# Two projections of a sparse-attention layer: from three 256-wide matmuls per weight block to one 512-wide and one 256-wide

## The chip, the cores and the metric

One core of a Trainium2 chip runs the kernel. The metric is the device time of one execution in microseconds; three runs of the kernel before took 584.46, 584.71 and 585.03 us, so the median is 584.71 us. All of a time's digits come from such runs or from one execution that was taken with the hardware profiler.

## The reference

The program is a two-layer decoder trunk on 256 tokens of width 1024, all in float32. Layer 0 is an mLSTM layer. Its output gives one set of keys and values, and layer 1 is a sparse-attention layer that reads them. The change touches only layer 1, which computes, for 16 heads of width 128:

```python
h = rmsnorm(x, norm_pre[1])                       # 256 x 1024
proj = h @ w_in                                   # w_in: 1024 x (2048 + 48 + 6144)
q = proj[..., :nqk] * DK ** -0.5                  # 16 heads x 128
gates = sigmoid(proj[..., nqk:nqk + ngl])         # 3 branches x 16 heads
zg = silu(proj[..., nqk + ngl:])                  # 3 branches x 16 heads x 128
# for each branch b (compressed, selected, window) and head:
s = q @ k_b.T - slope[head] * dist                # dist = query position - key position
p = softmax(where(mask, s, -inf))
o = sum over b of gates[b] * zg[b] * (p @ v_b)
x = x + rmsnorm(o @ w_out, norm_post[1])
```

Every matrix product has to keep float32 accuracy. The kernel gets it by splitting both operands into a high part `hi` (rounded to the matmul's own format, F32R) and a low part `lo` (the rest), and adding three products: hi x hi, hi x lo, lo x hi.

## The kernel before

**Tiles.** Activations are kept transposed. `hB` holds rmsnorm(x) for layer 1 as two tiles of 128 x 8 x 256, `hB_hi` and `hB_lo`: 8 blocks of 128 input features, 256 tokens. A projection (`proj_t`, L144) makes 256 output features, that is two halves m of 128, one for each head of a pair, in one PSUM tile `ps` of 128 x 2 x 256. It goes through 2 halves x 8 feature blocks, and for each block `mm3` (L135) issues three matmuls of 256 columns: weights hi with `hB_hi` (L137), weights hi with `hB_lo` (L138), weights lo with `hB_hi` (L139). That makes 48 matmuls a projection.

**Weights.** `w_chunk` (L141) fetches 512 KB by the SP queue into `raw` (4 buffers), ScalarE copies it to `whi` (L132, 5 buffers), VectorE subtracts to `wlo` (L133, 4 buffers). A projection uses two such chunks.

**Layer 1.** There are 8 pairs of heads p, and for each one q projection (`q_proj`, L807, its PSUM tile is `qps`) and three z projections (`z_branch`, L860, `zps`): 32 projections in all. The q and z of pair 0 are made early, among the work on keys and values; those of pair p + 1 are made while pair p goes through its scores, its transposes and its product with the values. On TensorE one pair is the sequence: scores of head 0 (`sps`, 9 matmuls), z projection, scores of head 1, z projection, q projection, 14 transposes of the probabilities (`ptc`, `pt`), z projection, product with the values (`oc`, `ob`, 13 matmuls). After the last pair the output projection (`acc`) follows.

**What follows a projection.** For z, ScalarE reads all 512 columns of `ps` and writes tanh(ps/2) to `zz` (L863); VectorE makes (zz + 1) * ps (L864). For q, ScalarE writes `qhi` (L811) and VectorE `qlo` (L812). A projection holds one of the 3 buffers of the pool `pj` until both are done.

**Softmax of one head** (`softmaxes`, L815). GpSimd makes a table `al` = -slope * dist of 128 x 800 for each head (L823, 2 buffers, 16 in all). VectorE adds it to each of six segments of scores and takes the maximum `mx` at the same time (L836), then `nm` = -mx (L839). ScalarE takes exp(e + nm) with its row sum `sm` (L844). VectorE makes the factors `rsm` (L846 to L849) and scales `e` (L857). The transposes read `e`.

**What sets the order.** The kernel is written with a tile framework: a scheduler puts the instructions of each engine in one list by priority and data dependences, and each engine works through its list in order. A waiting instruction therefore holds up all that stands behind it on its engine.

Of the kernel before, what the change touches and what calls it, by code (L numbers as in the profile page):

```python
# [7 lines left out]
F32 = mybir.dt.float32  # L8
# [7 lines left out]
P = 128  # L16
# [4 lines left out]
def trunk(ctx: ExitStack, tc: tile.TileContext, x, norm_pre, norm_post, a_w_in, a_conv_w, a_conv_b,  # L21
# [155 lines left out]
    def norm_t(t, rstd, gam, hT):  # L177

        n = tp.tile([P, D], F32, tag="tmp", name="nrm")
        for q in range(KT // 4):  # L180
# [63 lines left out]
    with ExitStack() as actx:  # L244
# [349 lines left out]
        for t, n in op.finish():  # L594
# [18 lines left out]
            if t == 0:  # L613
                hB = new_hT("hB")
# [5 lines left out]
    with ExitStack() as bctx:  # L620
# [25 lines left out]
        for c0, base in ((0, 0), (P + NB, 0), (W0, 0), (W0 + P, P), (W0 + 2 * P + NB, P), (W0 + 3 * P + NB, 0)):  # L646
            seg = dist[:, c0:c0 + P]
            nc.gpsimd.iota(seg, pattern=[[-1, P]], base=base, channel_multiplier=1,
                           allow_small_or_imprecise_dtypes=True)
            if base == 0:  # L650
                nc.gpsimd.affine_select(out=seg, in_=seg, pattern=[[-1, P]], compare_op=ALU.is_ge,
                                        fill=MASKED, base=0, channel_multiplier=1)
        for c0, base in ((P, 0), (W0 + 2 * P, P)):
            seg = dist[:, c0:c0 + NB]
            nc.gpsimd.iota(seg, pattern=[[-16, NB]], base=base, channel_multiplier=1,
                           allow_small_or_imprecise_dtypes=True)
            nc.gpsimd.tensor_scalar(seg, seg, -15.5, None, op0=ALU.add)
            nc.gpsimd.affine_select(out=seg, in_=seg, pattern=[[-16, NB]], compare_op=ALU.is_ge,
                                    fill=MASKED, base=base - 31, channel_multiplier=1)
# [116 lines left out]
        def branch_gates():  # L776
# [30 lines left out]
        def q_proj(p):  # L807
            ps = proj_t(bw, p * 256, hB, "qps")
            q = [qz.tile([P, 2, S], F32R, tag=f"q{s}", name=f"q{s}{p}") for s in ("hi", "lo")]
            sc = float(DK) ** -0.5  # L810
            nc.scalar.activation(q[0], ps, AF.Copy, scale=sc)  # L811
            nc.vector.scalar_tensor_tensor(q[1], ps, sc, q[0].bitcast(F32), op0=ALU.mult, op1=ALU.subtract)  # L812
            return q

        def softmaxes(p, q):  # L815
# [3 lines left out]
            for j in range(2):  # L819
                h = 2 * p + j  # L820
                al = b2.tile([P, W0 + KW], F32, tag="al", name=f"al{h}")
                with tc.issue_after(after_norm):
                    nc.gpsimd.tensor_scalar(al, dist, -slopes[h], None, op0=ALU.mult)  # L823
                e = E[:, j, :]
                mx = col(6, "mx")
                for t in range(NT):
# [203 lines left out]
```

## Time and profile before

| | us |
|---|---|
| median of 3 runs (lowest to highest) | 584.71 (584.46 to 585.03) |
| the profiled execution | 583.27 |
| its span, first to last instruction | 581.4 |
| TensorE busy (share of the span) | 568.1 (98%) |
| VectorE busy | 453.1 (78%) |
| ScalarE busy | 311.9 (54%) |
| GpSimd busy | 90.2 (16%) |

The profiled execution is 1.44 us below the median of the runs, and 1.87 us of it lie outside the span. The mean granted clock of TensorE was 0.996 of full speed. Matmuls overlap in the profile: a matmul of 256 columns is listed with about 0.28 us, but the next one starts about 0.12 us later, so what a matmul costs is read from start to start and not from its listed length. VectorE's instructions overlap by some 0.07 us in the same way. Layer 1's projections run from about 264 us on; from 311 us to 515 us seven pairs of heads follow one another, one in 29.1 us.

### The profile page before, as it was taken

How to read it: one execution, taken by the hardware profiler on the slowest of the kernel's cores; microseconds unless marked ns; L12 is line 12 of the kernel's file. 1: busy time of each engine (PE TensorE's matmuls, PEld its weight loads, DVE VectorE, ACT ScalarE, POOL GpSimd, SP SyncE). 2: the span in 40 equal slices, each digit the busy share in tenths (PEclk: the TensorE clock that was granted, in tenths of full speed). 3: DMA queues.
4: the chain of work that ended last, by engine and by line, in shares of the span. 5: the costliest groups of instructions: out<-in, count | busy, mean ns of one | idle time of the engine just before them, and what ended most of it. 6: DMA issues, size and time to landing. Idle time of an engine off the chain costs nothing.

```text
span 581.4 us, 10616 instructions
## 1 busy us (share of the span) xinstructions
PE 568.1 (98%) x4043; PEld 519.1 (89%) x4043; DVE 453.1 (78%) x944; ACT 311.9 (54%) x585; POOL 90.2 (16%) x104
## 2 busy tenths in 40 slices
PE   7998999999999999999999999999999999999995
PEld 3987987989999988879899999999999999998884
DVE  7689887486888876686635789888988998988663
ACT  6475675535544445463334574747474747475521
POOL 7610000201010040130003202021202121210000
PEclk9999999999999999999999999999999999999998
DMA  9984763253422447688995553636374636354501
GB/s 262 227 274 156 241 199 128 74 179 112 145 62 86 144 145 253 203 267 263 289 300 163 149 148 108 182 109 183 108 181 110 183 109 183 109 182 149 202 11 73
DMA packets 82693, 96.69 MB, mean 166 GB/s; under 512 B 4811, under 2 KB 68449, under 8 KB 82642
## 3 DMA queue, kind: packets, MB, share of 16 engines
q1 hardware_dynamic: 81040, 92.48, 52.0%
q0 software_dynamic: 1600, 3.52, 2.8%
q8 instruction: 32, 0.52, 0.4%
q14 instruction: 19, 0.16, 0.1%
q10 hardware_dynamic: 2, 0.00, 0.0%
HBM read 94.94 MB, written 1.05 MB: 165 GB/s over the span
## 4 chain that ended last, share of the span: by engine, by line
PE 90%; DVE 6%; issue 1%; DMA 1%; ACT 1%; POOL 0%; DVEq 0%; POOLq 0%; ACTq 0%
PE zps L137 11%; PE zps L139 11%; PE zps L138 11%; PE acc L137 5%; PE acc L138 5%; PE acc L139 5%; PE qps L138 3%; PE qps L137 3%; PE qps L139 3%; PE o L137 2%; PE o L138 2%; PE o L139 2%; PE pt L869 2%; DVE wlo L133 2%; PE xmps L139 1%; PE xmps L138 1%
## 5 line engine op out<-in xcount | busy, mean ns | idle before, releaser
L133 DVE TENSOR_TENSOR wlo<-raw,whi 128x1024 fp32r<-128x1024 f32 x150 | 181.6, 1222 | 62.5 <-PE zps L139 22.3
L132 ACT ACTIVATE whi<-raw 128x1024 fp32r<-128x1024 f32 x151 | 157.5, 1053 | 122.0 <-issue 27.1
L137 PE MATMUL zps<-hB_hi,whi 128*128 128x256 f32 x384 | 109.5, 285 | 0.0
L138 PE MATMUL zps<-hB_lo,whi 128*128 128x256 f32 x384 | 108.6, 283 | 0.0
L139 PE MATMUL zps<-hB_hi,wlo 128*128 128x256 f32 x384 | 108.6, 283 | 0.0
L823 POOL TENSOR_SCALAR al<-dist 128x800 f32<-128x800 f32 x16 | 42.4, 2647 | 209.8 <-DVE mx L836 159.6
L137 PEld LDWEIGHTS zps<-hB_hi,whi 128*128 128x128 f32 x384 | 73.5, 191 | 0.8 <-issue 0.8
L139 PEld LDWEIGHTS zps<-hB_hi,wlo 128*128 128x128 f32 x384 | 73.6, 192 | 0.0
L138 PEld LDWEIGHTS zps<-hB_lo,whi 128*128 128x128 f32 x384 | 73.6, 192 | 0.0
L844 ACT ACTIVATE e<-e,nm 128x16 f32<-128x16 f32 (+2 forms) x96 | 37.7, 394 | 16.3 <-DVE nm L839 15.9
L139 PE MATMUL xmps<-hA_hi,wlo 128*128 128x256 f32 x128 | 36.7, 287 | 3.5 <-DVE wlo L133 3.3
L137 PE MATMUL xmps<-hA_hi,whi 128*128 128x256 f32 x128 | 36.3, 283 | 0.5 <-ACT whi L132 0.5
L137 PE MATMUL zps<-hA_hi,whi 128*128 128x256 f32 x128 | 36.6, 286 | 0.0
L139 PE MATMUL zps<-hA_hi,wlo 128*128 128x256 f32 x128 | 36.4, 284 | 0.0
L138 PE MATMUL zps<-hA_lo,whi 128*128 128x256 f32 x128 | 36.3, 283 | 0.0
L137 PE MATMUL qps<-hB_hi,whi 128*128 128x256 f32 x128 | 36.2, 283 | 0.0
L138 PE MATMUL qps<-hB_lo,whi 128*128 128x256 f32 x128 | 36.2, 283 | 0.0
L139 PE MATMUL qps<-hB_hi,wlo 128*128 128x256 f32 x128 | 36.2, 283 | 0.0
L138 PE MATMUL xmps<-hA_lo,whi 128*128 128x256 f32 x128 | 36.2, 283 | 0.0
L139 PEld LDWEIGHTS xmps<-hA_hi,wlo 128*128 128x128 f32 x128 | 24.5, 191 | 4.5 <-DVE wlo L133 4.5
L137 PEld LDWEIGHTS xmps<-hA_hi,whi 128*128 128x128 f32 x128 | 24.5, 192 | 1.0 <-ACT whi L132 0.8
L137 PE MATMUL o<-whi,hA_hi 128*128 128x512 f32 x64 | 25.3, 395 | 0.0
(338 smaller groups left out, 1416.7 us busy)
## 6 DMA issues: line engine op xcount, KB each, us to landing
raw<-in_b_w_in_dram SPq DMA_DIRECT2D x64, 512.0 KB, 4.8
raw<-in_a_w_in_dram SPq DMA_DIRECT2D x48, 512.0 KB, 4.6
raw<-in_a_w_out_dram SPq DMA_DIRECT2D x16, 512.0 KB, 3.7
w<-in_cmp_w_dram SPq DMA_DIRECT2D x32, 256.0 KB, 6.6
raw<-in_b_w_out_dram SPq DMA_DIRECT2D x16, 512.0 KB, 3.6
raw<-in_kv_w_dram SPq DMA_DIRECT2D x8, 512.0 KB, 7.5
raw<-in_kv_w_dram SPq DMA_DIRECT2D x8, 256.0 KB, 3.7
x<-in_x_dram SPq DMA_DIRECT2D x4, 256.0 KB, 3.7
```

What stands on the lines that cost most here:

```text
L132: a = nc.scalar.activation(hi, src, AF.Copy)
L133: return a.ins, nc.vector.tensor_sub(lo, src, hi.bitcast(F32)).ins
L137: nc.tensor.matmul(dst, lhsT=l[0], rhs=r[0], start=start, stop=False)
L138: nc.tensor.matmul(dst, lhsT=l[0], rhs=r[1], start=False, stop=False)
L139: last_mm[0] = nc.tensor.matmul(dst, lhsT=l[1], rhs=r[0], start=False, stop=stop).ins
L823: nc.gpsimd.tensor_scalar(al, dist, -slopes[h], None, op0=ALU.mult)
L844: nc.scalar.activation(e[:, c0:c0 + n], e[:, c0:c0 + n], AF.Exp, bias=nm[:, i:i + 1], accum_out=sm[:, i:i + 1])
L869: nc.tensor.transpose(dst, E[:, j, c0:c0 + P], ident)
```

## The change

`hB` becomes two tiles by feature blocks instead of two tiles by part: `hB[q]` is 128 x 4 x 2 x 256, and for each feature block the high and the low part stand side by side as 512 columns. A new generator `proj_pairs` multiplies the high weights with all 512 columns in one matmul and then adds the low weights times the high part to the first 256. The PSUM tile of one half m now has 128 x 2 x 256: the first 256 columns hold hi x hi + lo x hi, the second hi x lo, and someone has to add the two. ScalarE copies the second to SBUF, VectorE adds the first. The generator hands out one half at a time, so each is evacuated by itself. z's last two steps go to GpSimd as a product and a sum. The q of each head is divided by the head's slope; then `dist` (now with its sign turned) can be added to the scores of every head, the multiplication by -slope is part of VectorE's reducing instruction, which takes a minimum, and `al` and the step from `mx` to `nm` are gone.

```diff
+    def proj_pairs(w, c0, hP, name):
+        ch = [w_chunk(w, 0, c0), w_chunk(w, 4, c0)]
+        for m in range(2):
+            ps = pjt([P, 2, S], name)
+            for c in range(2):
+                for k in range(4):
+                    l = [ch[c][i][:, k, m * P:(m + 1) * P] for i in range(2)]
+                    r = hP[c][:, k]
+                    nc.tensor.matmul(ps.rearrange("p i s -> p (i s)"), lhsT=l[0], rhs=r.rearrange("p i s -> p (i s)"),
+                                     start=c + k == 0, stop=False)
+                    last_mm[0] = nc.tensor.matmul(ps[:, 0], lhsT=l[1], rhs=r[:, 0], start=False,
+                                                  stop=c + k == 4).ins
+            yield m, ps
...
         def q_proj(p):
-            ps = proj_t(bw, p * 256, hB, "qps")
             q = [qz.tile([P, 2, S], F32R, tag=f"q{s}", name=f"q{s}{p}") for s in ("hi", "lo")]
-            sc = float(DK) ** -0.5
-            nc.scalar.activation(q[0], ps, AF.Copy, scale=sc)
-            nc.vector.scalar_tensor_tensor(q[1], ps, sc, q[0].bitcast(F32), op0=ALU.mult, op1=ALU.subtract)
+            for j, ps in proj_pairs(bw, p * 256, hB, "qps"):
+                sc = float(DK) ** -0.5 / slopes[2 * p + j]
+                qs = qz.tile([P, S], F32, tag="half", bufs=3, name="qs")
+                nc.scalar.activation(qs, ps[:, 1], AF.Copy)
+                nc.vector.tensor_add(qs, ps[:, 0], qs)
+                nc.scalar.activation(q[0][:, j, :], qs, AF.Copy, scale=sc)
+                nc.vector.scalar_tensor_tensor(q[1][:, j, :], qs, sc, q[0][:, j, :].bitcast(F32),
+                                               op0=ALU.mult, op1=ALU.subtract)
...
-                al = b2.tile([P, W0 + KW], F32, tag="al", name=f"al{h}")
-                with tc.issue_after(after_norm):
-                    nc.gpsimd.tensor_scalar(al, dist, -slopes[h], None, op0=ALU.mult)
...
-                        nc.vector.tensor_tensor_reduce(e[:, c0:c0 + n], src, al[:, c0:c0 + n], 1.0, -1e30,
-                                                       ALU.add, ALU.max, mx[:, 3 * t + b:3 * t + b + 1])
-                nm = col(6, "nm")
-                nc.vector.tensor_scalar(nm, mx, -1.0, None, op0=ALU.mult)
+                        nc.vector.tensor_tensor_reduce(e[:, c0:c0 + n], src, dist[:, c0:c0 + n], -slopes[h], 1e30,
+                                                       ALU.add, ALU.min, nm[:, 3 * t + b:3 * t + b + 1])
...
                         nc.scalar.activation(e[:, c0:c0 + n], e[:, c0:c0 + n], AF.Exp, bias=nm[:, i:i + 1],
-                                             accum_out=sm[:, i:i + 1])
+                                             scale=-1.0, accum_out=sm[:, i:i + 1])
...
         def z_branch(b, p):
-            ps = proj_t(bw, NQK + NGL + b * NQK + p * 256, hB, "zps")
             zz = qz.tile([P, 2, S], F32, tag="zz", bufs=6, name=f"zz{b}_{p}")
-            nc.scalar.activation(zz, ps, AF.Tanh, scale=0.5)
-            nc.vector.scalar_tensor_tensor(zz, zz, 1.0, ps, op0=ALU.add, op1=ALU.mult)
+            for j, ps in proj_pairs(bw, NQK + NGL + b * NQK + p * 256, hB, "zps"):
+                z = zz[:, j, :]
+                nc.scalar.activation(z, ps[:, 1], AF.Copy)
+                nc.vector.tensor_add(z, ps[:, 0], z)
+                th = qz.tile([P, S], F32, tag="half", bufs=3, name="zth")
+                nc.scalar.activation(th, z, AF.Tanh, scale=0.5)
+                nc.gpsimd.tensor_mul(th, th, z)
+                nc.gpsimd.tensor_add(z, z, th)
             return zz
```

The pieces left out make `hB` with the new shape (`new_pairs`, `norm_t`, `branch_gates`) and turn the sign of `dist`.

On TensorE and on the SP queue the order of the work stays the same, apart from the matmuls inside the 32 projections. On VectorE the list of a pair changes. This piece of the list before stands between the score maxima of head 1 and the transposes; `wlo` is a weight chunk's low part, `ec` and `e` are the scaled probabilities that the transposes read.

```order
L133 TENSOR_TENSOR wlo_4152<-raw_4149,whi_4151 128x1024
L839 TENSOR_SCALAR nm<-mx 128x6
L133 TENSOR_TENSOR wlo_4246<-raw_4243,whi_4245 128x1024
L133 TENSOR_TENSOR wlo_4252<-raw_4249,whi_4251 128x1024
L846 TENSOR_SCALAR sm<-sm 128x6
L848 RECIPROCAL rsm<-sm 128x6
L849 TENSOR_TENSOR rsm<-rsm,gs 128x6
L864 SCALAR_TENSOR_TENSOR zz_2_4139<-zz_2_4139,zps 128x512
L857 TENSOR_SCALAR ec_3933<-e_3932,rsm 128x3x16
L857 TENSOR_SCALAR e_3932<-e_3932,rsm 128x128 x2
L857 TENSOR_SCALAR ec_3933<-e_3932,rsm 128x3x16
L857 TENSOR_SCALAR e_3932<-e_3932,rsm 128x256 x2
```

The same place on VectorE now (lines of the changed file; L887 is the sum of a z half):

```order
L133 TENSOR_TENSOR wlo_4083<-raw_4080,whi_4082 128x1024
L868 TENSOR_SCALAR sm<-sm 128x6
L870 RECIPROCAL rsm<-sm 128x6
L887 TENSOR_TENSOR zz_2_4013<-zps,zz_2_4013 128x256
L871 TENSOR_TENSOR rsm<-rsm,gs 128x6
L133 TENSOR_TENSOR wlo_4169<-raw_4166,whi_4168 128x1024
L879 TENSOR_SCALAR ec_3881<-e_3880,rsm 128x3x16
L879 TENSOR_SCALAR e_3880<-e_3880,rsm 128x128 x2
L879 TENSOR_SCALAR ec_3881<-e_3880,rsm 128x3x16
L879 TENSOR_SCALAR e_3880<-e_3880,rsm 128x256 x2
L133 TENSOR_TENSOR wlo_4175<-raw_4172,whi_4174 128x1024
L887 TENSOR_TENSOR zz_2_4013<-zps,zz_2_4013 128x256
```

`nm` has left the list; of the three `wlo` ahead of `sm`, two now stand behind `rsm`, one of them behind the scaled `e`; and the `zz` of a whole projection has become two sums of halves, the second behind the scaled `e`. On ScalarE this is the list before from the exponentials of head 0 on; `whi` is a weight chunk's high part:

```order
L844 ACTIVATE e_4332,sm<-e_4332,nm 128x16
L844 ACTIVATE e_4332,sm<-e_4332,nm 128x128 x2
L844 ACTIVATE e_4332,sm<-e_4332,nm 128x16
L844 ACTIVATE e_4332,sm<-e_4332,nm 128x256 x2
L863 ACTIVATE zz_3_4435<-zps 128x512
L132 ACTIVATE whi_4551<-raw_4549 128x1024
L132 ACTIVATE whi_4645<-raw_4643 128x1024
L132 ACTIVATE whi_4651<-raw_4649 128x1024
```

and this the list now, where `zth` is the tanh of a half and waits for VectorE's sum of it:

```order
L866 ACTIVATE e_4250,sm<-e_4250,nm 128x16
L866 ACTIVATE e_4250,sm<-e_4250,nm 128x256 x2
L886 ACTIVATE zz_3_4288<-zps 128x256
L132 ACTIVATE whi_4452<-raw_4450 128x1024
L132 ACTIVATE whi_4538<-raw_4536 128x1024
L889 ACTIVATE zth<-zz_3_4288 128x256
L886 ACTIVATE zz_3_4288<-zps 128x256
L866 ACTIVATE e_4250,sm<-e_4250,nm 128x16
L889 ACTIVATE zth<-zz_3_4288 128x256
L866 ACTIVATE e_4250,sm<-e_4250,nm 128x128 x2
```

Where ScalarE had one instruction for a z projection it now has four, in two pairs, each with a VectorE instruction between its two. GpSimd's list loses its 16 `al` and gets 96 instructions of 128 x 256, a product and a sum for each of 48 z halves.

## Rows read from the trace of the kernel before

**Rows 1.** The page's busy times of the engines over the span.
```profile
PE 568.1 (98%) x4043; PEld 519.1 (89%) x4043; DVE 453.1 (78%) x944; ACT 311.9 (54%) x585; POOL 90.2 (16%) x104
```

**Rows 2.** The chain of waits, shares of the span by engine.
```profile
PE 90%; DVE 6%; issue 1%; DMA 1%; ACT 1%; POOL 0%; DVEq 0%; POOLq 0%; ACTq 0%
```

**Rows 3.** One pair: stretch, span, busy of PE, PEld, DVE, ACT, POOL, clock, DMA.
```profile
369.60:398.70 29.10, 29.10 (x240) 28.79 (x239) 26.00 (x67) 17.84 (x42) 5.58 (x2) 1.00 0.50 144
```

**Rows 4.** TensorE in order of time: start, listed length, line, output<-inputs, shape.
```profile
376.88 0.39 PE L137 MATMUL ob<-pt00hi,V0hi 128*128 128x512 f32 x1
...
377.58 0.28 PE L137 MATMUL ob<-pt1hi,V1hi 128*128 128x256 f32 x1
...
377.93 0.40 PE L137 MATMUL ob<-pt01hi,V0hi 128*128 128x512 f32 x1
...
378.64 0.28 PE L137 MATMUL ob<-pt1hi,V1hi 128*128 128x256 f32 x1
...
380.11 0.28 PE L137 MATMUL zps<-hB_hi,whi 128*128 128x256 f32 x1
...
385.86 0.29 PE L137 MATMUL sps<-KThi,qhi 128*128 128x272 f32 x1
...
558.05 0.39 PE L137 MATMUL acc<-whi,yThi 128*128 128x512 f32 x1
...
562.95 0.39 PE L137 MATMUL acc<-whi,yThi 128*128 128x512 f32 x1
```

**Rows 5.** Groups by line and shape: count, busy us, mean ns of one, idle before.
```profile
L864 DVE SCALAR_TENSOR_TENSOR zz<-zz,zps 128x512 f32<-128x512 f32 x24 | 16.3, 680 | 0.1
L839 DVE TENSOR_SCALAR nm<-mx 128x6 f32<-128x6 f32 x16 | 10.5, 657 | 0.1
L463 DVE SCALAR_TENSOR_TENSOR xc<-xc,vec,zth 128x256 f32<-128x256 f32 x16 | 7.7, 480 | 0.0
L812 DVE SCALAR_TENSOR_TENSOR qlo<-qps,qhi 128x512 fp32r<-128x512 f32 x8 | 5.5, 690 | 3.2 <-ACT qhi L811 3.2
L491 DVE TENSOR_TENSOR dd<-dps,cmask 128x256 f32<-128x256 f32 x4 | 1.7, 415 | 0.0
...
L863 ACT ACTIVATE zz<-zps 128x512 f32<-128x512 f32 x24 | 13.9, 578 | 0.0
L728 ACT ACTIVATE rs<-R 128x256 f32<-128x256 f32 x2 | 0.8, 378 | 1.0 <-PE R L721 1.0
```

**Rows 6.** VectorE in order of time, around work of GpSimd and away from it.
```profile
158.32 0.48 DVE L463 SCALAR_TENSOR_TENSOR xc<-xc,vec,zth 128x256 f32<-128x256 f32 x1
...
159.44 0.29 DVE L524 TENSOR_SCALAR rd<-rd 128x2 f32<-128x2 f32 x1
...
181.57 0.16 DVE L524 TENSOR_SCALAR rd<-rd 128x2 f32<-128x2 f32 x1
...
324.25 0.17 DVE L839 TENSOR_SCALAR nm<-mx 128x6 f32<-128x6 f32 x1
...
382.97 0.69 DVE L133 TENSOR_TENSOR ylowlo<-yacc,ylowhi 128x512 fp32r<-128x512 f32 x1
383.58 0.82 DVE L839 TENSOR_SCALAR nm<-mx 128x6 f32<-128x6 f32 x1
```

**Rows 7.** GpSimd in order of time at the same places.
```profile
158.47 1.23 POOL L470 TENSOR_TENSOR bd<-blk,bm 128x512 f32<-128x512 f32 x1 [18.95 <-PE kkps L478]
160.25 1.05 POOL L470 TENSOR_TENSOR bd<-blk,bm 128x512 f32<-128x512 f32 x1 [0.55 <-PE vps L485]
...
383.21 2.53 POOL L823 TENSOR_SCALAR al<-dist 128x800 f32<-128x800 f32 x1 [18.56 <-DVE mx L836]
```

**Rows 8.** What TensorE's transposes and value products wait for, in order of time.
```profile
374.14 0.69 DVE L133 TENSOR_TENSOR pt1lo<-pt,pt1hi 128x512 fp32r<-128x512 f32 x1
...
396.98 0.60 DVE L857 TENSOR_SCALAR e<-e,rsm 128x256 f32<-128x256 f32 x2
...
398.48 0.38 PE L879 MATMUL ptc<-ident,ec 128*96 128x128 f32 x2
```

More of the change, by code (lines that the diff above doesn't have):

```diff
@@ L186, in norm_t @@
                 last_tr[0] = nc.tensor.transpose(ps[:, k, :], n[:, (4 * q + k) * P:(4 * q + k + 1) * P], ident)
-            sl = (slice(None), slice(4 * q, 4 * q + 4), slice(t * P, (t + 1) * P))
-            evac = split(hT[0][sl], hT[1][sl], ps)
+            ts = slice(t * P, (t + 1) * P)
+            if len(hT[0].shape) == 4:
+                evac = split(hT[q][:, :, 0, ts], hT[q][:, :, 1, ts], ps)
+            else:
+                evac = split(*[a[:, 4 * q:4 * q + 4, ts] for a in hT], ps)
         return ins.ins, *evac
@@ L192, in new_hT, with new_pairs @@
         return [hp.tile([P, KT, S], F32R, tag="h8", name=f"{name}_{s}") for s in ("hi", "lo")]
+    def new_pairs(name):
+        return [hp.tile([P, KT // 2, 2, S], F32R, tag="h8", name=f"{name}_{q}") for q in range(2)]
+    def proj_pairs(w, c0, hP, name):
[11 more added lines that the diff above has]
+            yield m, ps
     class OutProj:
@@ L613, in trunk @@
             if t == 0:
-                hB = new_hT("hB")
+                hB = new_pairs("hB")
             with tc.issue_after(last_mm[0]):
@@ L647, in trunk @@
             seg = dist[:, c0:c0 + P]
-            nc.gpsimd.iota(seg, pattern=[[-1, P]], base=base, channel_multiplier=1,
+            nc.gpsimd.iota(seg, pattern=[[1, P]], base=-base, channel_multiplier=-1,
                            allow_small_or_imprecise_dtypes=True)
@@ L651, in trunk @@
                 nc.gpsimd.affine_select(out=seg, in_=seg, pattern=[[-1, P]], compare_op=ALU.is_ge,
-                                        fill=MASKED, base=0, channel_multiplier=1)
+                                        fill=-MASKED, base=0, channel_multiplier=1)
         for c0, base in ((P, 0), (W0 + 2 * P, P)):
             seg = dist[:, c0:c0 + NB]
-            nc.gpsimd.iota(seg, pattern=[[-16, NB]], base=base, channel_multiplier=1,
+            nc.gpsimd.iota(seg, pattern=[[16, NB]], base=-base, channel_multiplier=-1,
                            allow_small_or_imprecise_dtypes=True)
-            nc.gpsimd.tensor_scalar(seg, seg, -15.5, None, op0=ALU.add)
+            nc.gpsimd.tensor_scalar(seg, seg, 15.5, None, op0=ALU.add)
             nc.gpsimd.affine_select(out=seg, in_=seg, pattern=[[-16, NB]], compare_op=ALU.is_ge,
-                                    fill=MASKED, base=base - 31, channel_multiplier=1)
+                                    fill=-MASKED, base=base - 31, channel_multiplier=1)
         hsel = bp.tile([6 * NB, 2], F32, name="hsel")
@@ L786, in branch_gates @@
                 for i in range(2):
-                    nc.tensor.matmul(ps, lhsT=hl[:, k].rearrange("p i c -> p (i c)"), rhs=hB[i][:, k, :],
+                    nc.tensor.matmul(ps, lhsT=hl[:, k].rearrange("p i c -> p (i c)"), rhs=hB[k // 4][:, k % 4, i],
                                      start=k + i == 0, stop=k + i == KT)
@@ L820, in softmaxes @@
                 h = 2 * p + j
[L821 to L823 removed]
                 e = E[:, j, :]
[L825 removed]
+                nm = col(6, "nm")
                 for t in range(NT):
```

## The prediction

> **What bounds the kernel now.** I read the busy times first: TensorE works 98% of the span [rows 1]. That alone proves little, since listed lengths overlap, so the chain of waits comes next: 90% of what ended last runs through TensorE and 6% through VectorE [rows 2]. Then one pair of heads alone: in 29.10 us TensorE has no idle time, VectorE is busy 26.00, ScalarE 17.84, GpSimd 5.58, and TensorE's granted clock is 1.00, the 2.4 GHz level [rows 3]. So from about 311 to 515 us every 0.1 us less on TensorE is 0.1 us less in the end, as long as VectorE, which has only 3.1 us free in a pair, keeps up. The forecast turns on these two numbers. The clock cannot rise, and DMA is half used (0.50), so neither is an issue.
>
> **TensorE.** What a matmul costs is the step from one start to the next. A z projection goes from 380.11 to the scores' first matmul at 385.86: 5.75 us for 48, or 0.1198 us for 256 columns. From 558.05 to 562.95 lie 21 steps of 512 columns, 0.2333 us each [rows 4]. Weights hi times both parts now cost 0.2333 instead of 2 x 0.1198 = 0.2396: 0.0063 us less. There are 16 such places in a projection (8 blocks, 2 halves) and 32 projections: 512 x 0.0063 = 3.2 us. Thus dropping a third of the matmuls buys little, because a 512-column matmul takes 1.95 times as long as one of 256.
>
> The mixture of 512 and 256 is not in the projections of before, but it is in the value product, and it bounds the price. There three 512s take 377.58 - 376.88 = 0.70 and three 256s 377.93 - 377.58 = 0.35, so 0.2333 and 0.1167 [rows 4]. With that 256, a place saves 3 x 0.1198 - 0.2333 - 0.1167 = 0.0094 us, 4.8 us in all. Those 256 columns lie in two pieces, unlike the projections', so I stay near the first value and take 3.5 us. The lower bound is 2.4 us, with 0.235 for a 512: the second run of 512s there takes 378.64 - 377.93 = 0.71 us, and 0.235 is the mean step of the two runs. The other instructions of TensorE and their order stay.
>
> The Trainium skill, page "TensorE: Matmul & The Clock Gate", section "Back-to-back issue gap", gives N/2.4 + 2.5 ns for a warm matmul of N columns; by it a place saves only 2.5 ns, 1.3 us in all. The rows differ from it: both steps are longer than its 109 and 216 ns, and their difference of 0.1135 us for 256 columns is more than 107 ns. The sum above goes by the rows.
>
> **VectorE's own work, in one pair** [rows 5]. Gone: `nm`, twice 0.657; three `zz` at 0.680; one `qlo` at 0.690. Added: six z sums of 256 columns out of PSUM, for which `dd`, a sum of that shape out of PSUM, gives 0.415; two sums for q at 0.415; two `qlo` of 256 with both inputs in SBUF, for which `xc` gives 0.480. That is 2.49 + 0.83 + 0.96 - 1.31 - 2.04 - 0.69 = +0.24 us, and four more instructions than before (ten for six), each overlapping its neighbour by some 0.07: about nothing. The reducing instruction keeps its inputs and shapes; its multiplier was 1.0 and is now -slope, which I cost at nothing. So VectorE has about 26.0 us of work in a pair that lasts 29.1 - 4 x 0.11 = 28.7: 2.7 us are free.
>
> **GpSimd and what it does to VectorE.** This is where the change could fail. The trace shows the two engines holding each other up. `nm` took 0.17 us at 324.25, and 0.82 at 383.58, where `al` had been due since 383.21 and could start when `ylowlo` ended; the group's mean of 0.657 says that this is the usual case [rows 5 to 7]. `rd` took 0.29 at 159.44 with `bd` on GpSimd, and 0.16 at 181.57 without; `bd` itself took 1.23 instead of 1.05 because `xc` (158.32 to 158.80) was ahead of it [rows 6, 7]. So the hold of `bd`, with two inputs of 512 columns, lasts from about 158.66 (its start plus the 0.18 lost) to about 159.57 (`rd` delayed by 0.13 from 159.44): 0.91 us of its 1.05. A GpSimd product of two inputs of 256 columns then holds for half of that, 0.45 us, and takes perhaps 0.6. Twelve come in a pair, 5.4 us of holds; the two `al` go, whose cost to VectorE was in `nm` and is already counted.
>
> How many of the twelve land on VectorE? What the rows show held up, or holding, has all its operands in SBUF: `nm`, `rd`, `xc`, `ylowlo`. I take it that the others, which read PSUM, neither hold nor wait. `wlo`, the scaling of `e`, `yacc`, `ylowlo` and the new `qlo` are of the first kind, more than half of VectorE's pair. A half's product on GpSimd starts about 0.9 us after its sum began (the sum's 0.415, a tanh of about 0.4, two hand-offs), the second instruction 0.65 later. Going through VectorE's new list: behind z half 1 of the first branch stand maxima (0 to 0.4 lost), behind half 0 the scaling of `e` (0.2 to 0.8), behind the second branch's halves `wlo` and scaling, then q's sum and `wlo` (0.6 to 1.8), behind the third branch's `wlo`, then value products (0.2 to 0.8). Sum 1.0 to 3.8, middle 2.4 us, against 2.7 free. This just fits.
>
> The Trainium skill, page "SBUF — State Buffer", section "Who interferes with whom", has the rule: a VectorE instruction with two SBUF inputs, or in a mode that uses both ports, and a GpSimd instruction that reads SBUF exclude each other for the whole instruction. The trace agrees on who is held up, not on how long: `al` is listed with 2.53 us and delayed `nm` by 0.65. By the rule taken whole, twelve of 0.6 us would be 7.2 us a pair.
>
> **Where lateness would show.** If VectorE falls behind, TensorE does not stop at once. The transposed probabilities are ready at 374.83 and used at 377.58, 2.7 us later [rows 4, 8]. The transposes start at 398.48, when `e` is scaled at 397.58, 0.9 us before [rows 8]; without `nm` and with a `wlo` moved behind the scaling this becomes longer by over 2 us. PSUM: three buffers now hold halves, so a half must be evacuated within the two half projections after it, 5.7 us, where it had two whole ones. By the durations above, the sum of a half comes up in VectorE's list at most some 4 us after its matmuls. Weights are split about a projection ahead. About 2.5 us of lag are free, then each us of lag is one of TensorE.
>
> **ScalarE.** In place of 0.578 for z and about the same for q come four instructions near 0.38 (`rs`, 256 columns out of PSUM) [rows 5]: +0.94 us for each of four projections, 17.84 to 21.6 us of 28.7. It is hidden beside TensorE. What waits behind a tanh that waits for VectorE's sum is the next `whi`, with a projection's time to spare. SP's queue keeps its order. `al` made no one wait in the chain, so its going gains nothing beyond `nm`.
>
> **Sum.** The profiled execution took 583.27 us; 3.5 less is 579.8. The median of the runs lies 1.44 above that execution, so 584.71 - 3.5 = 581.2 us.
>
> **Rivals.**
> 1. *The holds land more often and VectorE becomes the bound (slower).* Its place is a pair's `wlo` and scaling behind z sums. At the upper 3.8 us a pair lasts 26.0 + 3.8 = 29.8, 1.1 over TensorE's 28.7; over seven pairs 7.7, less 2.5 of free lag, 5.2 us of stalls, against 3.5 gained: 586.4. It decides where the stalls reach the 3.5 gained, (3.5 + 2.5) / 7 = 0.86 us a pair over the 2.7 free: 3.6 us of holds, two thirds of the 5.4. For it: VectorE is already busy 89% of a pair [rows 3], and its list has `wlo` or scaling behind most sums. Against it: two thirds must land, though the other half of its work neither holds nor waits. Chance 0.19.
> 2. *A matmul of 512 gains next to nothing over two of 256 (no change or a little faster).* If a 512 between 256s costs what it did in the second run of the value product, 0.71 / 3 = 0.2367, and the 256 stays at 0.1198, a place saves 0.0029 us, 1.5 us in all: 583.2 [rows 4]. Against it stand the 21 steps of 0.2333. The page of the Trainium skill on TensorE comes out close to this rival, as said above. Chance 0.12.
> 3. *Hand-offs eat it up.* Each half passes ScalarE, VectorE, ScalarE and GpSimd through lists worked in order. Half a us lost in each of seven pairs is 3.5 us: 584.7. For it: four waits where there was one; against it: the spare times above. Chance 0.11.
>
> The forecast itself, 579.9 to 582.3 by the two bounds of the saving, has 0.58. Three runs of this kernel spread over 0.1%, so 0.2%, 1.2 us, is what can be told from no change: 583.5 and 585.9 are the borders. Faster: the forecast, half of rival 2, a little of rival 3, 0.65. Same: half of rival 2, most of rival 3 and a little of rival 1, 0.18. Slower: 0.17. The range reaches from 579.6 to rival 1's 586.4.
>
> **What the new profile would show.** Right: a projection's 32 matmuls in about 5.64 us from first to next; a pair in about 28.7; TensorE without gaps in it; GpSimd's products near 0.6 us; single `wlo` and scalings of `e` longer by up to 0.45 where a product runs, VectorE near 28 us in a pair. Wrong: idle time of TensorE ahead of `ob`, `sps` or a first matmul of a half with VectorE as the releaser, and a pair at 29.1 or more (rival 1 or 3); or a step of 0.355 and over for a 512 with its 256 (rival 2).

## The result, and the profile after

The changed kernel takes 593.31 us (592.15 to 593.62, four runs) where the kernel before took 584.87 in the same session: a ratio of 1.0141, with a 95% interval of 1.0127 to 1.0154. It is 8.4 us slower. The forecast was 581.2, and its range ended at 586.4. The profiled execution has a span of 591.6 us.

The page's busy times and chain of waits, against [rows 1, 2]:

```profile
PE 566.3 (96%) x3531; PEld 492.1 (83%) x3531; DVE 472.7 (80%) x976; ACT 335.8 (57%) x681; POOL 151.5 (26%) x184
...
PE 78%; DVE 9%; DMA 5%; ACT 3%; issue 3%; POOL 2%; DVEq 0%; POOLq 0%; SPq 0%; ACTq 0%
```

TensorE has 512 matmuls less and is still busy for 566 us. Its share of the chain fell from 90% to 78%; what it lost went to VectorE, ScalarE and DMA (DMA's pieces of the chain all lie outside the stage that is slower). So the loss must be waits of TensorE, and it lies in one stage: from the first `oc` to the last there were 208.2 us before (347.5 to 555.7) and 217.5 now (348.4 to 565.9), 9.3 more. Two of the seven pairs and the mean of five, against [rows 3] (stretch, span, busy of PE, PEld, DVE, ACT, POOL, clock, DMA):

```profile
379.00:409.20 30.20, 28.86 (x175) 25.25 (x173) 28.06 (x72) 20.68 (x54) 12.65 (x12) 1.00 0.48 135
409.20:439.80 30.60, 29.17 (x175) 25.52 (x175) 28.46 (x72) 20.96 (x55) 12.85 (x12) 1.00 0.51 142
...
sum 151.80, PE 144.72 PEld 126.88 DVE 141.10 ACT 104.10 POOL 63.91; mean PE 28.94 PEld 25.38 DVE 28.22 ACT 20.82 POOL 12.78
```

A pair takes 151.80 / 5 = 30.36 us instead of 29.10, and TensorE has gaps in it. The view of waits for 330 to 560 us has ScalarE's longest waits for VectorE and these gaps of TensorE (engine, line, releaser: us in total, times, longest):

```profile
ACT zth L889 <- DVE zz L887: 41.8, 22, 3.2
...
PE sps L137 <- DVE yacc L938: 9.7, 7, 1.4
```

TensorE has one wait in each pair, about 1.4 us, always at the same place: the third group of score matmuls waits for VectorE's product `yacc` at L938, which frees the PSUM buffer of `oc`. The same view of the kernel before has no wait of TensorE for `yacc`. The chain around one of these waits, in order of time (start, us, what):

```profile
379.17 0.59 DVE pt1lo L133
379.76 0.34 DVE zz L887
...
380.18 0.06 ACT zth L889
...
380.51 1.05 ACT whi L132
...
381.58 1.32 DVE wlo L133
382.90 0.61 DVE yacc L938
...
383.56 0.39 PE sps L137
```

VectorE comes late to `zz`; ScalarE's tanh waits for it, with `whi` behind; VectorE's `wlo` waits for `whi`, with `yacc` behind; and TensorE waits for `yacc`. No line of the view of waits names GpSimd as what an engine waited for. On VectorE, what was slowed in this stretch (330 to 560 us) is read from the groups by line and shape (count, busy us, mean ns), beside those of e1 further down:

```profile
L133 DVE TENSOR_TENSOR wlo<-raw,whi 128x1024 fp32r<-128x1024 f32 x64 | 79.3, 1242 | 7.4 <-PE acc L138 4.5 <-ACT whi L132 2.6 <-issue 0.4
L887 DVE TENSOR_TENSOR zz<-zps,zz 128x256 f32<-128x256 f32 x41 | 16.7, 408 | 0.0
L879 DVE TENSOR_SCALAR e<-e,rsm 128x256 f32<-128x256 f32 x30 | 14.1, 511 | 0.0
L946 DVE TENSOR_TENSOR yacc<-yacc,ytmp 128x512 f32<-128x512 f32 x14 | 13.0, 932 | 0.0
...
L945 DVE TENSOR_TENSOR ytmp<-ob,zz 128x512 f32<-128x512 f32 x14 | 9.5, 676 | 0.0
L837 DVE SCALAR_TENSOR_TENSOR qlo<-qs,qhi 128x256 fp32r<-128x256 f32 x14 | 9.4, 668 | 0.5 <-ACT qhi L836 0.5
```

### The profile page after: what moved, and what is told of

The parts are those of the page before. It is cut to its first block, busy times and chain, and to the rows that moved or that the text cites. A ratio compares the mean times of both kernels' runs of the same rounds, so it can differ in the third digit from the quotient of the medians.

```text
span 591.6 us, 9801 instructions
## 1 busy us (share of the span) xinstructions
PE 566.3 (96%) x3531; PEld 492.1 (83%) x3531; DVE 472.7 (80%) x976; ACT 335.8 (57%) x681; POOL 151.5 (26%) x184
## 4 chain that ended last, share of the span: by engine, by line
PE 78%; DVE 9%; DMA 5%; ACT 3%; issue 3%; POOL 2%; DVEq 0%; POOLq 0%; SPq 0%; ACTq 0%
PE zps L210 13%; PE zps L212 6%; PE acc L137 5%; PE acc L138 5%; PE acc L139 5%; PE qps L210 4%; DVE wlo L133 3%; PE zps L139 3%; PE zps L138 3%; PE zps L137 3%; PE qps L212 2%; PE o L137 2%; PE o L138 2%; PE o L139 2%; PE pt L896 1%
## 5 line engine op out<-in xcount | busy, mean ns | idle before, releaser
L210 PE MATMUL zps<-hB,whi 128*128 128x512 f32 x384 | 136.3, 397 | 0.0
L212 PE MATMUL zps<-hB,wlo 128*128 128x256 f32 x384 | 107.6, 280 | 0.0
L890 POOL TENSOR_TENSOR zth<-zth,zz 128x256 f32<-128x256 f32 x48 | 42.9, 893 | 174.9 <-ACT zth L889 174.9
L210 PEld LDWEIGHTS zps<-hB,whi 128*128 128x128 f32 x384 | 72.1, 188 | 16.8 <-issue 0.4
L212 PEld LDWEIGHTS zps<-hB,wlo 128*128 128x128 f32 x384 | 72.5, 189 | 0.0
L891 POOL TENSOR_TENSOR zz<-zz,zth 128x256 f32<-128x256 f32 x48 | 57.8, 1205 | 3.8
L889 ACT ACTIVATE zth<-zz 128x256 f32<-128x256 f32 x48 | 19.9, 415 | 47.7 <-DVE zz L887 46.3
L210 PE MATMUL qps<-hB,whi 128*128 128x512 f32 x128 | 45.3, 396 | 0.0
L212 PE MATMUL qps<-hB,wlo 128*128 128x256 f32 x128 | 35.9, 280 | 0.0
L210 PEld LDWEIGHTS qps<-hB,whi 128*128 128x128 f32 x128 | 24.0, 188 | 5.7
```

Source lines behind the costliest of these rows:

```text
L210: nc.tensor.matmul(ps.rearrange("p i s -> p (i s)"), lhsT=l[0], rhs=r.rearrange("p i s -> p (i s)"), start=c + k == 0, stop=False)
L212: last_mm[0] = nc.tensor.matmul(ps[:, 0], lhsT=l[1], rhs=r[:, 0], start=False, stop=c + k == 4).ins
L889: nc.scalar.activation(th, z, AF.Tanh, scale=0.5)
L890: nc.gpsimd.tensor_mul(th, th, z)
L891: nc.gpsimd.tensor_add(z, z, th)
```

## The experiments

Three theories stood at the start. Hold: GpSimd's gate instructions (the product and sum of each z half) hold VectorE's, that is, VectorE's instructions take longer while they run, and VectorE has no room for it. Hand-offs: ScalarE and VectorE wait for one another in their fixed orders. Buffer: the one PSUM buffer of `oc` is the only tight place. A fourth, that GpSimd's gate simply arrives too late, came up after the first runs. All results, with the mean pair read from `oc` to `oc` over four or five pairs:

| run | GpSimd, instr. a pair | kernel us | ratio to before (95%) | pair us | VectorE busy | TensorE busy |
|---|---|---|---|---|---|---|
| before | 2 (`al`) | 584.9 | | 29.10 | 25.9 | 29.10 |
| changed | 12 | 593.3 | 1.0127–1.0154 | 30.36 | 28.2 | 28.94 |
| e1 no GpSimd, no gate | 0 | 579.4 | 0.989–0.993 | 28.50 | 25.5 | 28.50 |
| e3 gate on VectorE | 0 | 580.4 | 0.990–0.993 | 28.48 | 27.1 | 28.48 |
| e10 as e3, one GpSimd instr. a half whose result nobody reads | 6 | 585.4 | 0.999–1.002 | 29.06 | 28.5 | 28.73 |
| e9 as e3, two of them | 12 | 603.6 | 1.029–1.036 | 31.40 | 30.7 | 29.54 |
| e18 changed, GpSimd's gate on half the columns | 12 | 579.9 | 0.990–0.993 | 28.46 | 26.2 | 28.46 |
| e12 changed, no scaling of 256 | 12 | 586.6 | 1.002–1.005 | 29.74 | 26.7 | 28.86 |
| e15 as e3, gate twice on VectorE | 0 | 591.1 | 1.008–1.014 | 30.84 | 28.9 | 29.42 |
| e17 branch 2's gate on VectorE | 8 | 584.7 | 0.999–1.002 | 29.30 | 27.6 | 28.79 |
| e16 branch 3's gate on VectorE | 8 | 607.1 | 1.034–1.041 | 32.38 | 29.7 | 30.03 |
| e14 tanh ahead of the sum | 12 | 592.5 | 1.011–1.015 | 30.30 | 28.6 | 28.95 |
| e5 tanh from PSUM behind the sum | 12 | 594.6 | 1.014–1.018 | 30.55 | 28.3 | 29.11 |
| e4 six and two PSUM buffers | 12 | 597.8 | 1.020–1.024 | 30.68 | 28.0 | 28.87 |
| e2 table of distances alone | 0 | 584.1 | 0.998–1.001 | 29.10 | 24.8 | 29.10 |

**e1: the GpSimd work left out.**

```diff
...
                 nc.scalar.activation(th, z, AF.Tanh, scale=0.5)
-                nc.gpsimd.tensor_mul(th, th, z)
-                nc.gpsimd.tensor_add(z, z, th)
...
```

> The changed kernel without the two GpSimd instructions of each z half: the product (tanh+1)*z is left out, z's plain sum takes the place of the gate. Kernel before 584.9 us, changed kernel 593.3. Theory A (port): VectorE is late because GpSimd's 12 instructions in a pair hold it; without them VectorE is as before, about 26 us of a pair's 28.7 on TensorE, the third score group of a head no longer waits for the product at L938, a pair falls from 30.2 to about 28.7 us, the kernel to 581 to 583 us. Theory B (hand-offs): the lateness comes from ScalarE and VectorE waiting for one another in their fixed orders (sum, tanh, whi, wlo); these stay, so a pair stays at 29.8 or more and the kernel at 590 to 593 us. Both together: 585 to 589.

Measured: 579.41 us. Everything lost came back, and the saving on top: this is the "hold" side, and better than its 581 to 583. In the trace VectorE goes through a pair in the same order as in the changed kernel, so the difference of its busy time is what GpSimd does to it: 28.2 - 25.5 = 2.7 us a pair. The groups of this run show on which instructions it lay:

```profile
L133 DVE TENSOR_TENSOR wlo<-raw,whi 128x1024 fp32r<-128x1024 f32 x67 | 81.7, 1222 | 15.8 <-PE acc L138 6.5 <-PE zps L212 3.9 <-PE qps L212 2.8
L887 DVE TENSOR_TENSOR zz<-zps,zz 128x256 f32<-128x256 f32 x40 | 16.5, 412 | 0.3
L944 DVE TENSOR_TENSOR yacc<-yacc,ytmp 128x512 f32<-128x512 f32 x16 | 11.0, 689 | 0.1
L943 DVE TENSOR_TENSOR ytmp<-ob,zz 128x512 f32<-128x512 f32 x16 | 10.9, 682 | 0.1
...
L879 DVE TENSOR_SCALAR e<-e,rsm 128x256 f32<-128x256 f32 x30 | 9.0, 343 | 0.0
...
L837 DVE SCALAR_TENSOR_TENSOR qlo<-qs,qhi 128x256 fp32r<-128x256 f32 x14 | 5.8, 417 | 0.5 <-ACT qhi L836 0.5
```

The scaling of `e` falls from 511 to 343 ns, the sum into `yacc` from 932 to 689, `qlo` from 668 to 417: all operands in SBUF. `wlo`, the longest of this kind, falls only from 1242 to 1222. The z sum (408 and 412) and `ytmp` (676 and 682), which read PSUM, show no hold.

**e3: the gate on VectorE.**

```diff
-                nc.gpsimd.tensor_mul(th, th, z)
-                nc.gpsimd.tensor_add(z, z, th)
+                nc.vector.scalar_tensor_tensor(z, th, 1.0, z, op0=ALU.add, op1=ALU.mult)
```

> The changed kernel with z's product as one VectorE instruction, (tanh+1)*z, for each half instead of two on GpSimd. Per pair six instructions of about 0.4 us more on VectorE (2.4 us), and GpSimd's holds (estimated at 2.3 us a pair) gone. Theory A (port): what VectorE gains from the holds it gives for its own work, so the time stays at 591 to 595 us. Theory B (hand-offs): VectorE's added 2.4 us come on top of hand-offs that stay, 593 to 598 us.

Measured: 580.38 us, faster than both kernels (ratio to before 0.9916, 0.9901 to 0.9931). Both expectations missed. VectorE does 1.6 us a pair more than in e1, and TensorE never waits:

```profile
376.50:405.10 28.60, 28.60 (x175) 25.39 (x174) 27.14 (x79) 21.05 (x55) 0.00 (x0) 1.00 0.52 148
```

So 27.1 us of VectorE's own work fit into 28.5 in this order of the list; 28.2 with holds did not in the changed kernel's. That left open whether it is the holds or the lateness of GpSimd's result; e9 and e10 separate these.

**e9 and e10: GpSimd works beside e3 for nobody** (e10 without the second line).

```diff
                 nc.vector.scalar_tensor_tensor(z, th, 1.0, z, op0=ALU.add, op1=ALU.mult)
+                nc.gpsimd.tensor_mul(th, th, z)
+                nc.gpsimd.tensor_add(th, th, z)
```

> The kernel with z's product on VectorE (580.4 us, VectorE busy 27.1 of a pair's 28.4), and beside it GpSimd does a product and a sum of the same shape for each z half, whose result nobody reads. Theory A (hold): VectorE's instructions with SBUF operands only wait while GpSimd's run; the traces put these holds at 3.0 us a pair, so VectorE comes to 30.1 of 28.4 and a pair to 30.3 to 31.5 us, the kernel to 594 to 602 us. Theory C (late gate): what cost the time was that GpSimd's result came some 1.5 us later than VectorE's would; nobody waits for it here, so the time stays at 580 to 582 us.

> The same with one such GpSimd instruction for each z half, the product alone. Theory A (hold): half of the holds, 1.5 us a pair, VectorE at 28.6 of 28.4: a pair at 28.7 to 29.8 us, the kernel at 582 to 590 us. Theory C (late gate): 580 to 582 us.

Measured: 603.58 us, 1.6 over hold's 594 to 602, and 585.36 us, within its 582 to 590. Nobody waits for these results, VectorE's order in a pair is e3's, and the kernel loses 5.0 us with six instructions a pair and 23.2 with twelve. So holds cost time without any late gate, and since no engine of the changed kernel waits for GpSimd, the late gate falls. VectorE's busy time rises by 1.4 and 3.6 us a pair, and the time more than in proportion: from e10 to e9 VectorE has 2.3 us more and the pair 2.3 us more (a part of it is TensorE's clock, see the end). e9's wait is the changed kernel's, only longer:

```profile
PE sps L137 <- DVE yacc L939: 12.7, 7, 2.4
```

VectorE's sum alone does not give the pair: e10 has more of it than the changed kernel (28.5 and 28.2 us) and a shorter pair (29.06 and 30.36), because in its order of the list VectorE stands idle 0.6 us a pair instead of 2.1.

**e12: VectorE relieved, GpSimd untouched.**

```diff
-                        nc.vector.tensor_scalar(dst, src, rs[:, i:i + 1], None, op0=ALU.mult)
+                        if n < 2 * P:
+                            nc.vector.tensor_scalar(dst, src, rs[:, i:i + 1], None, op0=ALU.mult)
```

> The changed kernel, GpSimd's work as it is, with the scaling of the 256 wide parts of the exponentials left out (four VectorE instructions a pair, 0.343 us each without a hold, 0.511 with them). Theory A (hold): VectorE falls from 28.3 us a pair by 1.4 us and is no longer behind, though the holds fall on other instructions: 580 to 586 us. Theory C (late gate): GpSimd's gate is as late as before, 591 to 593 us.

Measured: 586.56 us, 6.8 less than the changed kernel, 0.6 over "hold"'s 580 to 586. GpSimd's gate was as late as before, so this too speaks against the late gate. But with 26.7 us of VectorE, less than in e3, TensorE still waited at `yacc` (5.8 us in seven waits, 9.7 in the changed kernel). A sum over the pair is not the whole of it. Nor is e12's list just the changed one with four instructions less: a `wlo` and a `qlo` stand at other places in it.

**e16 and e17: the same work on both engines, at another place** (e17 with `b == 1`).

```diff
-                nc.gpsimd.tensor_mul(th, th, z)
-                nc.gpsimd.tensor_add(z, z, th)
+                if b == 2:
+                    nc.vector.scalar_tensor_tensor(z, th, 1.0, z, op0=ALU.add, op1=ALU.mult)
+                else:
+                    nc.gpsimd.tensor_mul(th, th, z)
+                    nc.gpsimd.tensor_add(z, z, th)
```

> The changed kernel with the product on VectorE for the third z branch alone (the projection just ahead of the values, two of the pair's six halves), on GpSimd for the other two. VectorE gives up about 1.0 us of holds and does 0.84 us itself. If VectorE's sum over a pair decides: 591 to 594 us. If it decides where the holds fall, and those just ahead of the product at L938 are the ones that count: 582 to 588 us.

> The same for the second z branch alone (the projection behind the second half of the scores, far ahead of the values). If VectorE's sum over a pair decides: 591 to 594 us, as for the third branch. If the place decides: 590 to 594 us here and clearly less for the third branch.

Measured: 607.06 us for e16 and 584.72 for e17. The place decides, but the other way round than I expected. Both kernels have the same instructions, in lists of another order, and VectorE is busy 29.7 us a pair in one and 27.6 in the other. In e16 ScalarE's tanhs come together, and GpSimd's instructions run beside a series of short scalings on VectorE. There, first GpSimd's rows, then VectorE's, each in order of time (start, us, engine, line, output<-inputs, shape):

```profile
460.17 0.73 POOL L893 TENSOR_TENSOR zth<-zth,zz 128x256 f32<-128x256 f32 x1 [20.37 <-ACT zth L889]
460.98 0.75 POOL L894 TENSOR_TENSOR zz<-zz,zth 128x256 f32<-128x256 f32 x1
461.69 0.73 POOL L893 TENSOR_TENSOR zth<-zth,zz 128x256 f32<-128x256 f32 x1
...
460.15 0.80 DVE L879 TENSOR_SCALAR ec<-e,rsm 128x48 f32<-128x48 f32 x1
460.87 0.94 DVE L879 TENSOR_SCALAR e<-e,rsm 128x128 f32<-128x128 f32 x2
461.74 0.74 DVE L879 TENSOR_SCALAR ec<-e,rsm 128x48 f32<-128x48 f32 x1
```

and in e17, around a `wlo` and at the same scalings without GpSimd:

```profile
438.81 1.60 POOL L894 TENSOR_TENSOR zz<-zz,zth 128x256 f32<-128x256 f32 x1
...
438.44 1.38 DVE L133 TENSOR_TENSOR wlo<-raw,whi 128x1024 fp32r<-128x1024 f32 x1 [0.31 <-ACT whi L132]
...
454.89 0.25 DVE L879 TENSOR_SCALAR ec<-e,rsm 128x48 f32<-128x48 f32 x1
455.06 0.47 DVE L879 TENSOR_SCALAR e<-e,rsm 128x128 f32<-128x128 f32 x2
455.44 0.25 DVE L879 TENSOR_SCALAR ec<-e,rsm 128x48 f32<-128x48 f32 x1
```

Beside short instructions GpSimd keeps its 0.73 us and VectorE pays, `ec` 0.80 instead of 0.25. Beside a `wlo` that began first, GpSimd pays, 1.60 instead of 0.75, and `wlo` takes 1.38 instead of 1.22. By an estimate the same GpSimd work costs VectorE 1.5 us a pair in e17 and 3.6 in e16: its own list would be 25.5 (e1) and a third of e3's extra 1.6, 26.05, taken from 27.6 and 29.7.

**e15: VectorE's own work instead of holds.**

```diff
                 nc.vector.scalar_tensor_tensor(z, th, 1.0, z, op0=ALU.add, op1=ALU.mult)
+                nc.vector.scalar_tensor_tensor(th, th, 1.0, z, op0=ALU.add, op1=ALU.mult)
```

> The kernel with z's product on VectorE (580.4 us, VectorE 27.1 us of a pair's 28.4) and that product made once more on VectorE for each z half, into a tile that nobody reads: 2.5 us a pair, no GpSimd work. If what counts is how full VectorE is, whatever fills it: 29.6 us and the waits that are left, a pair of 30.0 to 31.0 us, the kernel at 591 to 598 us. If GpSimd's instructions cost in another way than by VectorE's time: 580 to 584 us.

Measured: 591.14 us, at the low end of the range for a VectorE filled by whatever it may be. The time is like that of the holds, but the waits are not: none at `yacc`, but at projections for `wlo`, 5.5 us in seven waits, the longest 2.0, and weights arrive late as well (`whi` waits 25.7 us for DMA between 330 and 560 us). So this run shows that a fuller VectorE costs time, not that it does so in the changed kernel's way.

**e5 and e14: the hand-off at tanh.** e5 lets tanh read PSUM, e14 also puts it ahead of the sum (the edit shown); both leave the product of `h`'s low part out of tanh's argument.

```diff
-                nc.vector.tensor_add(z, ps[:, 0], z)
                 th = qz.tile([P, S], F32, tag="half", bufs=3, name="zth")
-                nc.scalar.activation(th, z, AF.Tanh, scale=0.5)
+                nc.scalar.activation(th, ps[:, 0], AF.Tanh, scale=0.5)
+                nc.vector.tensor_add(z, ps[:, 0], z)
```

> The changed kernel with z's tanh reading the hi part of the sum straight from PSUM, so that ScalarE no longer waits for VectorE's sum there (the product of h's low part is left out of tanh's argument; the sum itself is still made and multiplied). GpSimd's work stays as it is. Theory A (port): little changes, 591 to 593 us. Theory B (hand-offs): ScalarE's 46 us of waits for the sum go, the weights' high parts come in time, and most of the 8.4 us come back, 584 to 587 us, or less with TensorE's own saving on top.

> The changed kernel with z's tanh ahead of VectorE's sum, reading the hi part from PSUM (the product of h's low part is left out of tanh's argument). In the run with tanh reading PSUM behind the sum, ScalarE still waited for the sum (41 us in all); here it cannot. GpSimd's work is unchanged. If holds alone make VectorE late: 590 to 594 us, VectorE busy 28 us a pair as before. If the hand-offs between ScalarE and VectorE alone do it: 580 to 585 us. If both add up to the lateness: 585 to 590 us.

Measured: 594.58 and 592.47 us. e5 is over both of its ranges and decides nothing: ScalarE waited for the sum as before, 40.9 us; why it did, though tanh no longer reads the sum, was not traced. In e14 that wait is gone, and the kernel is at 592.5, as "hold alone" had it; VectorE is at 28.6 us, with the holds on `wlo` (1369 ns) and `ec` (431) instead. ScalarE's waits reappear in front of `e` and `qhi`:

```profile
ACT e L866 <- DVE nm L860: 39.8, 29, 3.2
ACT qhi L836 <- DVE qs L835: 15.1, 7, 2.4
```

The hand-offs carry the lateness; they are not its source.

**e4: one more buffer at the tight place, one less for the projections.** The last two lines only place the output projection's sums.

```diff
-    pj = ctx.enter_context(tc.tile_pool(name="pj", bufs=3, space=bass.MemoryType.PSUM))
-    wk = ctx.enter_context(tc.tile_pool(name="wk", bufs=5, space=bass.MemoryType.PSUM))
+    pj = ctx.enter_context(tc.tile_pool(name="pj", bufs=2, space=bass.MemoryType.PSUM))
+    wk = ctx.enter_context(tc.tile_pool(name="wk", bufs=6, space=bass.MemoryType.PSUM))
...
-            self.acc = [[(wkt if t + n == 2 else pjt)([P, 512], f"acc{t}{n}") for n in range(2)] for t in range(NT)]
+            self.acc = [[(wkt if t == 1 else pjt)([P, 512], f"acc{t}{n}") for n in range(2)] for t in range(NT)]
```

> The changed kernel with one PSUM buffer moved from the projections' pool to the pool of scores, transposes and values (6 and 2 instead of 5 and 3). If the place where lateness reaches TensorE is the buffer that the product at L938 gives back to the third score group, one buffer more gives it about 1.3 us more of slack and the stalls of 1.4 us in each pair go: 583 to 587 us. If VectorE (or the chain of hand-offs) is late as a whole, the stall only moves to the next buffer or to the transposes' low parts: 591 to 594 us. Two projection buffers could also stop TensorE at a projection's start: then the trace shows waits there and the time is over 593.

Measured: 597.75 us. The wait at `yacc` is gone, and another took its place, at q's projection for the z sum:

```profile
PE qps L210 <- DVE zz L887: 13.3, 8, 1.8
```

That is the third case of the expectation: the projections' pool, now with two buffers, stops TensorE. So the wait at `yacc` is that of the buffer, but what one more there would give by itself this run does not show; six beside three for the projections were not tried.

**e2: the table of distances alone.** The projections are as before; q is scaled by head in two halves. Part of the edit, against the kernel before:

```diff
...
-                        nc.vector.tensor_tensor_reduce(e[:, c0:c0 + n], src, al[:, c0:c0 + n], 1.0, -1e30,
-                                                       ALU.add, ALU.max, mx[:, 3 * t + b:3 * t + b + 1])
-                nm = col(6, "nm")
-                nc.vector.tensor_scalar(nm, mx, -1.0, None, op0=ALU.mult)
+                        nc.vector.tensor_tensor_reduce(e[:, c0:c0 + n], src, dist[:, c0:c0 + n], -slopes[h], 1e30,
+                                                       ALU.add, ALU.min, nm[:, 3 * t + b:3 * t + b + 1])
...
```

> The kernel before with one part of the change alone: the scores share one table of distances, q is scaled by head. The projections and the gate of z are as before. TensorE does the same work and is busy all of a pair's 29.1 us in the kernel before; VectorE loses two negations and their holds, 1.3 us a pair. Expected by all theories: no change, 584 to 585.5 us. If the holds by the tables already cost the kernel before something, 581 to 583 us.

Measured: 584.11 us, no change, as expected: VectorE falls to 24.8 us a pair and TensorE is busy through all 29.10. This part neither gains nor loses.

**e18: the same list, GpSimd's instructions half as long.** e12 and e16 left open whether the length of the holds decides or only their place.

```diff
-                nc.gpsimd.tensor_mul(th, th, z)
-                nc.gpsimd.tensor_add(z, z, th)
+                nc.gpsimd.tensor_mul(th[:, 0:P], th[:, 0:P], z[:, 0:P])
+                nc.gpsimd.tensor_add(z[:, 0:P], z[:, 0:P], th[:, 0:P])
```

> The changed kernel with GpSimd's two gate instructions on the first 128 columns of each z half alone (the gate of the other 128 is left out). Number, place and hand-offs of all instructions stay, only GpSimd's lengths fall to about half. If the length of the holds decides (2.7 us a pair, about half of it here): VectorE 26.8 to 27.1 us a pair, which fitted in the kernel with the gate on VectorE, 580 to 584 us. If it is the place, a GpSimd instruction in the way of certain VectorE ones whatever its length: 589 to 593 us.

Measured: 579.91 us, 13.4 less than the changed kernel. Number, hand-offs and, in the trace, the order of VectorE's instructions in a pair are the same, and TensorE has no gap left:

```profile
376.50:405.10 28.60, 28.60 (x176) 25.40 (x175) 26.39 (x72) 20.91 (x55) 8.97 (x13) 1.00 0.52 148
```

VectorE is busy 26.2 us a pair (mean of five): 0.7 us of holds, where whole lengths gave 2.7. Twelve instructions at the same places are carried when they are short, so it is the length of the holds, and no certain place alone, that stops TensorE. e1, e18 and the changed kernel thus differ in GpSimd's instructions alone, none, half and whole: pairs of 28.50, 28.46 and 30.36 us.

## Why the prediction was wrong, by its steps

- **TensorE: right.** "Weights hi times both parts now cost 0.2333 instead of 2 x 0.1198 = 0.2396". TensorE in the changed kernel, the second and the sixteenth place of one projection, then the first and the sixteenth of the next:

```profile
373.75 0.40 PE L210 MATMUL zps<-hB,whi 128*128 128x512 f32 x1
...
378.61 0.39 PE L210 MATMUL zps<-hB,whi 128*128 128x512 f32 x1
...
384.02 0.40 PE L210 MATMUL zps<-hB,whi 128*128 128x512 f32 x1
...
389.31 0.40 PE L210 MATMUL zps<-hB,whi 128*128 128x512 f32 x1
```

  The second has 15 steps in 5.29 us, 0.353 a place; three steps of 0.1198 were 0.359. That saves 0.0067, close to the 0.0063 of the sum. The first has 14 steps in 4.86, 0.347, and some whole projections go at that step too; why is open. Where TensorE does not wait, e3 shows the term: most of its projections take 5.64 us from the first matmul to the next group, as forecast, some 5.56; a pair takes 28.48 instead of 29.10, and 5.0 us are saved in all, for the 3.5 taken and the bound of 4.8.
- **VectorE's own work: near.** I had about 26.0 us a pair; e1 has 25.5.
- **The holds: right in size, in part by luck.** "Sum 1.0 to 3.8, middle 2.4 us": measured 2.7, and VectorE busy 28.2 for my "near 28". That PSUM readers are not held was right too. But the prediction put a large part of the holds on `wlo`, which lost 0.02 us each (1242 and 1222 ns); they fell on the scaling, `yacc` and `qlo`. A half's product and sum took GpSimd 0.90 and 1.22 us in the mean instead of "near 0.6". The Trainium skill, page "SBUF — State Buffer", section "Who interferes with whom", says that whoever issues first keeps the shared ports for its whole instruction. The trace agrees in e17, where `wlo` was 0.37 us ahead and GpSimd paid; in e16 the starts of `ec` and GpSimd lie within 0.05 us of each other, so who was first cannot be read there. The 7.2 us a pair that the prediction worked out from the rule, with all of it on VectorE, stand against 2.7.
- **"This just fits" and "About 2.5 us of lag are free": the steps that failed.** Two things were wrong there. First, VectorE does not fill a pair: in the changed kernel it stands idle 2.1 us a pair (30.36 - 28.22), nearly all of it in waits for ScalarE in its own list, and still 0.6 to 0.7 in e9 and e10. 28.2 of 28.7 left 0.5 us for that, and the prediction took all that was free as usable. Second, the lag. I looked at the transposes and the projections' buffers, not at the buffer of `oc`. In the kernel before, TensorE and VectorE there, in order of time:

```profile
376.65 0.39 PE L910 MATMUL oc<-ptc,vc 96*128 96x512 f32 x1
...
378.05 0.68 DVE L911 TENSOR_TENSOR yacc<-oc,zz 128x512 f32<-128x512 f32 x1
...
379.76 0.28 PE L137 MATMUL sps<-KThi,qhi 128*128 128x256 f32 x1
```

  `yacc` ended at 378.73, and the third score group began at 379.76: 1.0 us were free, not 2.5 (0.6 in one of seven pairs). `yacc` started 1.40 us after `oc`; in the changed kernel it was 3.87 (378.96 to 382.83), so VectorE came 2.5 us later, and 1.4 of it became a wait in every pair. Nor was it a one-off credit to be set against all seven pairs, as rival 1 had it.
- **The rivals.** Rival 1 had the mechanism, VectorE behind through the holds, but set its threshold at 3.6 us of holds and its price at 586.4. 2.7 were enough, for 593.3. Rival 3's hand-offs are in the chain, but only where VectorE is already late (e1, e14, e18). Rival 2, a step of 0.2367 + 0.1198 = 0.357 and 1.5 us in all, is refuted by the 0.353 and by e3's 5.0 us.
- **ScalarE and DMA.** ScalarE was 20.8 us a pair for my 21.6; between 330 and 560 us no wait of TensorE names it or a transfer.

The sum, from e3's side: 585.4 - 5.0 = 580.4 for the idea itself, then + 12.9 for putting the gate on GpSimd.

What is not settled is why a pair of e12, with 26.7 us of VectorE, still stalls where e3 with 27.1 and e18 with 26.2 do not. Its GpSimd instructions have their full length, so single holds near `yacc` are likely, and the order of its list differs, but no run moved either alone.

## What to carry to other kernels

Where a change hands work from an engine with room to GpSimd, price what GpSimd holds up on VectorE as well as the work itself: here 0.42 us of VectorE's own time for each half was cheaper than two GpSimd instructions "for free". Count an engine with a fixed order as full before its busy time equals the bound, since its own waits come on top, and by how much depends on its order (here 27.1 of 28.5 us passed in e3, 26.7 did not in e12); and look for the first buffer that its lateness blocks. For that, list for each PSUM buffer the gap between the end of its last reader and the start of its next writer; the smallest gap is the slack.

## What the runs showed of the hardware that was not expected

The granted clock fell after some of the long waits of TensorE. In e16 TensorE waited 1.83 us ahead of 483.55; the row of that wait and the windows around it (stretch, span, busy, clock in the column before the DMA share):

```profile
483.55 0.39 PE L137 MATMUL sps<-KThi,qhi 128*128 128x256 f32 x1 [1.83 <-DVE yacc L941]
...
482.00:484.00 2.00, 0.45 (x3) 0.45 (x4) 2.00 (x4) 0.47 (x3) 0.00 (x0) 1.00 0.51 105
484.00:486.00 2.00, 2.00 (x9) 1.71 (x8) 2.00 (x6) 0.68 (x3) 0.00 (x0) 0.52 0.96 252
486.00:488.00 2.00, 2.00 (x9) 1.70 (x8) 1.95 (x11) 1.57 (x6) 0.00 (x0) 0.63 0.55 159
488.00:490.00 2.00, 2.00 (x14) 1.74 (x13) 0.69 (x4) 1.67 (x8) 0.00 (x0) 1.00 0.04 13
```

The clock is 0.52, close to the 1.2 GHz level, right behind the wait, and back at 1.00 from 488. A pair with this lasts 32.8 and 32.9 us, the pairs without it 31.9. Not every such wait does this: one of 1.83 us ahead of 451.68 in the same run left the clock at 1.00, and so did those of 1.8 us in e4; what decides it is open. In the changed kernel, with waits of up to 1.4 us, all five pairs have 1.00. So a part of the steep rise from e10 to e9 (one pair of e9 is at 0.95) is the clock and not VectorE.
